# Pool mixer of a hybrid encoder layer: its weights folded into the input projection on the chip, the running means stored directly

## The chip, the cores and the metric

The kernel runs on one core of one Trainium2 chip, in one launch. The metric is device time in microseconds (us), as the median of several runs; the profile shows one more execution, with its own time. A core has five engines that the text names: TensorE (PE, with its weight loads PEld), VectorE (DVE), ScalarE (ACT), GpSimd (POOL) and SyncE (SP), which only issues transfers here. They run side by side and wait for each other through semaphores.

## What is computed

One layer on 16 + 1024 tokens of width 1024. A normalised input goes through one input projection, whose columns feed three mixers: a pool mixer (256 columns, four groups of 64, windows 2, 4, 8 and 16), forgetting attention (six heads) and stick-breaking attention (six heads). Their outputs are joined, pass an output projection, and a SwiGLU block follows. The pool mixer, which the change is about, is this:

```python
def multiscale_pool_mixer(u, pool_w, pool_scale):
    ...
    window_sum = cs - cs0[:, lo, jnp.arange(N_POOL_GROUPS)[None, :]]
    mean = window_sum / (t1 - lo).astype(jnp.float32)[None, :, :, None]
    d = (mean - ug).astype(u.dtype)
    mixed = jnp.einsum('blgc,gcd->blgd', d, pool_w)
    return mixed.reshape(b, l, POOL_WIDTH) * pool_scale
```

Here u is the projection's first 256 columns, u = a @ w_in[:, :256], and the running mean and the difference act along the tokens, each column for itself. So mixing the columns with pool_w, a 64 x 64 matrix per group, can be done after the running mean or before it.

## The kernel before

All large products run in a split form: each operand is kept as a high part (rounded to the matmul's input type, float32r) and a low part (the rest), and three matmuls (high x high, high x low, low x high) stand for one. A weight block of 128 output columns comes in four parts of 128 x 2 x 128: `wpart` (L158) loads one from DRAM over SP's queue (tile wr), POOL writes the high part (wh, through `hi_pool`, L76) and, for this part of the kernel, POOL also subtracts to get the low part (wl, L164). The tags wh and wl have five buffers each (WB = 5). `proj_piece` (L283) projects up to 512 tokens with 24 matmuls into PSUM (tag mm, two buffers), eight steps of the contraction times three.

Two streams are interleaved by hand. `attention` goes through six pairs of heads (the first stick-breaking, then three forgetting, then two stick-breaking), and `filler` gives TensorE work beside it: for each next pair the projections of its keys, queries and values (`project`, L365). In front of the projections for pairs 2 and 4 (POOLS, L847) it runs `pool_pieces` (L597) for one half of the pool mixer, two groups of 64 columns. Every step of a stream yields a planned cost, and `interleave` (L788) brings the filler to a goal (a sum of such costs) by the end of each pair. Both streams only write a program order; the planner of the tile framework then fixes each engine's order by that priority and by when, in its own time model, operands and buffers come free. The attention has its priority raised by 300 instructions (BOOST, L846).

One half of the pool mixer goes like this. The four weight parts are loaded; pw, a 128 x 128 tile of tag e, is cleared (L601), gets two 64 x 64 blocks of pool_w by transfer (L603), and is split into pwh (ACT, L605) and pwl (VectorE, L607). Then for four pieces of 248 to 264 tokens: projection into PSUM; u = projection times the row factor rbc (VectorE, L627), with 16 tokens of overlap carried along by POOL (L626, L630); the window sums by repeated doubling (VectorE, L639), each level in a new buffer of tag e; mean minus u, one instruction for each group of 64 partitions (VectorE, L647), into tag r; its high part on POOL and its low part on VectorE (L652). One piece later `mix` follows: three matmuls with pwh, pwl (L612 to L614), a copy on ACT that applies the pool scale (L616), and the store of the result to DRAM from ACT's queue (L617). Tags e and r have three buffers each; the stick-breaking attention (`sb_scores`, L442) uses the same two tags for every piece of its scores.

Of the kernel before, what the change touches and what calls it, by code (L numbers as in the profile page):

```python
# [8 lines left out]
F32 = mybir.dt.float32  # L9
# [7 lines left out]
KD = 8  # L17
NM = 16
# [12 lines left out]
def hymba_trunk(  # L31
# [5 lines left out]
    w_fl: bass.AP,  # L37
    fbias: bass.AP,
    pool_w: bass.AP,
    pool_scale: bass.AP,  # L40
# [77 lines left out]
    psc = cst.tile([128, 2], F32, name="psc")  # L118
    nc.scalar.dma_start(psc, pool_scale)
    fb = cst.tile([6, 1], F32, name="fb")  # L120
    nc.scalar.dma_start(fb, fbias)
# [35 lines left out]

    def wpart(c, hf):  # L158
        raw = T(r1, [128, 2, 128], F32, "wr", 4)
        nc.sync.dma_start(raw, w_in[c, :, 2 * hf:2 * hf + 2, :])  # L160
        wh = T(r1, [128, 2, 128], F32R, "wh", WB)
        hi_pool(wh, raw)
        wl = T(r1, [128, 2, 128], F32R, "wl", WB)
        WPE[0].tensor_tensor(wl, raw, wh, ALU.subtract)  # L164
        return wh, wl
# [6 lines left out]
    def wload(c):  # L172
        return wflat([wpart(c, hf) for hf in range(4)])
# [422 lines left out]

    def pool_pieces(ci):  # L597

        w = wload(ci)
        pw = T(ap_, [128, 512], F32, "e", 3)[:, :128]  # L600
# [5 lines left out]
        pwl = T(ap_, [128, 128], F32R, "pwl")  # L606
        V.tensor_tensor(pwl, pw, pwh, ALU.subtract)  # L607
        late = []

        def mix(s0, n, dh, dl):  # L610
            p = mm("mm", [128, 512], MMB)
            PE.matmul(p[:, :n], pwh, dh[:, :n], start=True, stop=False)  # L612
            PE.matmul(p[:, :n], pwh, dl[:, :n], start=False, stop=False)
            PE.matmul(p[:, :n], pwl, dh[:, :n], start=False, stop=True)  # L614
            yo = T(ap_, [128, 512], F32, "e", 3)
            S.activation(yo[:, :n], p[:, :n], AF.Copy, scale=psc[:, ci:ci + 1])  # L616
            nc.scalar.dma_start(ysd[ci][:, s0:s0 + n], yo[:, :n])  # L617

        last = T(ap_, [128, NM], F32, "last")
        for t0, m in ((0, 264), (248, 280), (512, 272), (768, 272)):  # L620
# [4 lines left out]
            if t0:  # L625
                G.tensor_copy(u[:, :NM], last)  # L626
            V.tensor_tensor(u[:, c0:m], o[0][:, :m - c0], rbc[:, t0 + c0:t0 + m], ALU.mult)  # L627
            if t0 + m < L:
                last = T(ap_, [128, NM], F32, "last")
                G.tensor_copy(last, u[:, m - NM:m])  # L630

            lv = []
            cur = u
            for lev in range(4 if ci else 2):
                sft = 1 << lev
                st = 2 * sft - 1
                nx = T(ap_, [128, 512], F32, "e", 3)
                lo = 64 if lev == (3 if ci else 1) else 0
                V.tensor_tensor(nx[lo:128, st:m], cur[lo:128, st:m], cur[lo:128, st - sft:m - sft], ALU.add)  # L639
                cur = nx  # L640
                lv.append(nx)
            n = m - NM
            dd = T(ap_, [128, 512], F32, "r", 3)
            for g in range(2):
                win = 2 << (2 * ci + g)
                r = slice(64 * g, 64 * g + 64)
                V.scalar_tensor_tensor(dd[r, :n], lv[-2 + g][r, NM:m], 1.0 / win, u[r, NM:m],  # L647
                                       ALU.mult, ALU.subtract)
            dh = T(ap_, [128, 512], F32R, "r", 3)
            hi_pool(dh[:, :n], dd[:, :n])  # L650
            dl = T(ap_, [128, 512], F32R, "r", 3)
            V.tensor_tensor(dl[:, :n], dd[:, :n], dh[:, :n], ALU.subtract)  # L652
            while late:
                mix(*late.pop())
            late.append((t0, n, dh, dl))
            yield 0.5
        while late:
            mix(*late.pop())
        yield 0.5

# [519 lines left out]
```

## Time and profile before

| | |
|---|---|
| median of 3 runs | 1284.89 us (1284.74 to 1286.3) |
| profiled execution | 1286.02 us, of which the span of the trace is 1284.2 us |
| busy time in the span | PE 1215.3 us, PEld 1023.5, DVE 947.2, ACT 630.5, POOL 480.2 |
| granted TensorE clock, mean | 0.982 of full speed |
| transfers | 147.13 MB, on average 115 GB/s |

All rows come from the one profiled execution. Times in its rows count from the start of the span. A matmul's busy time overlaps the next one's, so the distance from one start to the next is its price where they follow closely. The granted clock is TensorE's: 1 is 2.4 GHz, and its lower level is half of that, 1.2 GHz; a stretch's number is the mean over it.

### The profile page before, as it was taken

How to read it: one execution, taken by the hardware profiler on the slowest of the kernel's cores; microseconds unless marked ns; L12 is line 12 of the kernel's file. 1: busy time of each engine (PE TensorE's matmuls, PEld its weight loads, DVE VectorE, ACT ScalarE, POOL GpSimd, SP SyncE). 2: the span in 40 equal slices, each digit the busy share in tenths (PEclk: the TensorE clock that was granted, in tenths of full speed). 3: DMA queues.
4: the chain of work that ended last, by engine and by line, in shares of the span. 5: the costliest groups of instructions: out<-in, count | busy, mean ns of one | idle time of the engine just before them, and what ended most of it. 6: DMA issues, size and time to landing. Idle time of an engine off the chain costs nothing.

```text
span 1284.2 us, 18471 instructions
## 1 busy us (share of the span) xinstructions
PE 1215.3 (95%) x6310; PEld 1023.5 (80%) x6310; DVE 947.2 (74%) x1713; ACT 630.5 (49%) x1318; POOL 480.2 (37%) x534
## 2 busy tenths in 40 slices
PE   7699899999898989999898999999999999999997
PEld 5587778888788878778687888888888888788885
DVE  8667886868977779997777676666767656876557
ACT  6456754645448677767743333332223334444443
POOL 6459046362363764550105453443544410000001
PEclk9999899999899989999999999999999999999999
DMA  5100011010100161201505554445544439565653
GB/s 180 40 17 27 13 47 34 26 42 18 50 29 30 38 213 67 74 25 50 197 25 180 171 167 151 138 136 181 189 164 160 136 131 344 172 212 199 197 173 139
DMA packets 73146, 147.13 MB, mean 115 GB/s; under 512 B 9052, under 2 KB 21340, under 8 KB 73052
## 3 DMA queue, kind: packets, MB, share of 16 engines
q1 hardware_dynamic: 69728, 142.01, 33.3%
q10 hardware_dynamic: 3324, 3.95, 0.9%
q8 instruction: 50, 0.82, 0.3%
q14 instruction: 44, 0.36, 0.1%
HBM read 103.98 MB, written 41.94 MB: 114 GB/s over the span
## 4 chain that ended last, share of the span: by engine, by line
PE 66%; DVE 11%; issue 4%; ACT 4%; DMA 2%; POOL 1%; SPq 0%; DVEq 0%; POOLq 0%; ACTq 0%
PE s L890 21%; PE mm L289 10%; PE mm L890 8%; PE s L1075 7%; PE mm L701 4%; PE o L511 4%; PE mm L1075 3%; PE o L1075 3%; PE s L531 3%; DVE r L470 3%; PE s L429 1%; PE s L431 1%; DVE x L703 1%; DVE P L472 1%; DMA raw<-in_w_down 1%
## 5 line engine op out<-in xcount | busy, mean ns | idle before, releaser
L890 PE MATMUL s<-t,wh 128*128 128x512 f32 x544 | 170.4, 392 | 3.5 <-ACT wh L876 3.5
L890 PEld LDWEIGHTS s<-t,wh 128*128 128x128 f32 x544 | 102.7, 189 | 25.7 <-ACT wh L876 4.2
L890 PE MATMUL s<-s,wh 128*128 128x512 f32 x384 | 118.5, 390 | 0.0
L876 ACT CAST wh<-ss 128x512 fp32r<-128x512 f32 x80 | 49.5, 621 | 133.6 <-PE s L890 93.0
L890 PE MATMUL s<-t,wl 128*128 128x512 f32 x272 | 106.3, 391 | 0.0
L289 PE MATMUL mm<-x,wh 128*128 128x512 f32 (+1 forms) x320 | 100.1, 387 | 1.1 <-DVE pt L354 1.1
L538 ACT CAST ph<-s 128x512 fp32r<-128x512 f32 (+2 forms) x168 | 70.7, 434 | 60.0 <-PE s L531 23.9
L890 PE MATMUL mm<-t,wh 128*128 128x512 f32 x320 | 98.5, 389 | 0.0
L1063 ACT CAST wh<-sg 128x512 fp32r<-128x512 f32 x74 | 46.0, 623 | 104.6 <-PE s L1075 46.1
L876 ACT CAST wh<-raw 128x512 fp32r<-128x512 f32 x68 | 41.7, 621 | 111.2 <-PE s L890 72.4
L539 DVE TENSOR_TENSOR pl<-s,ph 128x512 fp32r<-128x512 f32 (+2 forms) x168 | 81.1, 492 | 19.9 <-ACT ph L538 17.5
L1064 DVE TENSOR_TENSOR wl<-sg,wh 128x512 fp32r<-128x512 f32 x74 | 51.0, 690 | 56.9 <-ACT wh L1063 56.6
L511 PE MATMUL o<-pl,v 128*128 128x256 f32 (+1 forms) x288 | 85.8, 314 | 0.7 <-DVE pl L521 0.6
L511 PE MATMUL o<-ph,v 128*128 128x256 f32 (+1 forms) x288 | 80.2, 292 | 3.8 <-ACT ph L520 2.4
L890 PEld LDWEIGHTS s<-s,wh 128*128 128x128 f32 x384 | 71.9, 188 | 14.9
L984 DVE TENSOR_TENSOR cg<-s,tmp 128x512 f32<-128x512 f32 x60 | 41.2, 687 | 56.9 <-PE s L890 56.9
L1114 POOL TENSOR_TENSOR r<-r,mhalf 128x1 f32<-128x1 f32 x8 | 4.4, 547 | 209.0 <-DVE r L1113 207.4
L289 PE MATMUL mm<-xa,wh 128*128 128x264 f32 (+3 forms) x248 | 78.5, 320 | 1.2 <-ACT rbc L239 0.7
L289 PE MATMUL mm<-xa,wl 128*128 128x264 f32 (+3 forms) x248 | 76.5, 313 | 1.2 <-POOL wl L164 1.2
L289 PE MATMUL mm<-xb,wh 128*128 128x264 f32 (+3 forms) x248 | 77.0, 313 | 0.0
L531 PE MATMUL s<-ident,P 128*128 128x128 f32 x432 | 68.8, 278 | 6.3 <-DVE pl L521 3.6
L878 DVE TENSOR_TENSOR wl<-ss,wh 128x512 fp32r<-128x512 f32 x80 | 68.7, 862 | 8.2 <-ACT wh L876 6.8
(287 smaller groups left out, 3636.6 us busy)
## 6 DMA issues: line engine op xcount, KB each, us to landing
sg<-lsd SPq DMA_DIRECT2D x70, 256.0 KB, 3.2
raw<-in_w_gate SPq DMA_DIRECT2D x22, 512.0 KB, 5.4
raw<-in_w_up SPq DMA_DIRECT2D x22, 512.0 KB, 3.9
wr<-in_w_in SPq DMA_DIRECT2D x80, 128.0 KB, 2.2
raw<-in_w_down SPq DMA_DIRECT2D x20, 512.0 KB, 3.6
lsd<-cg SPq DMA_DIRECT2D x40, 256.0 KB, 3.2
raw<-rsd SPq DMA_DIRECT2D x40, 256.0 KB, 3.4
raw<-in_w_down SPq DMA_DIRECT2D x34, 256.0 KB, 3.1
```

The source lines that it names most:

```text
L289: PE.matmul(p[:, :n], w[k][ww], xx(k, t0, n), start=i == 0, stop=i == 23)
L511: PE.matmul(po[:, c:256], pr.v[h][:, kb, :], x, start=first and ix == 0, stop=(kb == nkb - 1 and ix == 1), skip_group_check=True)
L531: PE.transpose(tp[:, gi, ii, :], ptiles[ii][:, kc], ident)
L538: S.copy(ph[:, a:b], tpf[:, a:b])
L539: V.tensor_tensor(pl[:, a:b], tpf[:, a:b], ph[:, a:b], ALU.subtract)
L701: PE.matmul(p, y_[:, ts_], w_[:, ds], start=i == 0, stop=i == 3 * len(ws) - 1)
L876: S.copy(wh, a)
L878: V.tensor_tensor(wl, a, wh, ALU.subtract)
L890: PE.matmul(p, ws[ww][:, k, :], xs_[xx][:, k, :], start=first and i == 0, stop=i == 11, skip_group_check=True)
L1063: S.copy(wh, a)
L1064: V.tensor_tensor(wl, a, wh, ALU.subtract)
L1075: PE.matmul(p, x[xx][:, 128 * b:128 * b + 128], y[yy], start=first and i == 0, stop=last and i == 2, skip_group_check=True)
```

## The change

The pool weights are multiplied into the projection's weights on the chip, once per half, before anything is projected. For that the host lays the first 256 columns of w_in down a second time, turned (w_pt: the 128 columns of a half on the partitions). `pool_weights` loads the four turned parts with `wpart`, splits them as before, and multiplies each 128 x 128 block with the split block-diagonal pw: 24 matmuls of 128 columns. ACT and VectorE split the products from PSUM into the wh and wl parts that `proj_piece` takes. The pieces then project straight to the mixed columns. The pool scale is applied in the first step on u. The last doubling, which only the upper 64 partitions need, is done in place, read and written backwards. One instruction with a per-partition reciprocal width (invw, four small fills at the start) gives mean minus u for all 128 partitions, and its result, in tag r, is stored from ACT's queue one piece later. The mixing matmuls, the split of their input (POOL and VectorE) and ACT's copies go.

```diff
+    invw = cst.tile([128, 2], F32, name="invw")
+    for ci in range(2):
+        for g in range(2):
+            V.memset(invw[64 * g:64 * g + 64, ci:ci + 1], 1.0 / (2 << (2 * ci + g)))
...
-    def wpart(c, hf):
+    def wpart(c, hf, src=None):
         raw = T(r1, [128, 2, 128], F32, "wr", 4)
-        nc.sync.dma_start(raw, w_in[c, :, 2 * hf:2 * hf + 2, :])
+        nc.sync.dma_start(raw, (w_in if src is None else src)[c, :, 2 * hf:2 * hf + 2, :])
...
-    def pool_pieces(ci):
-
-        w = wload(ci)
+    def pool_weights(ci):
+
         pw = T(ap_, [128, 512], F32, "e", 3)[:, :128]
         V.memset(pw, 0.0)
         for g in range(2):
...
         V.tensor_tensor(pwl, pw, pwh, ALU.subtract)
+        parts = []
+        for q in range(2):
+            turned = [wpart(ci, 2 * q + i, w_pt) for i in range(2)]
+            p = mm("mm", [128, 512], MMB)
+            for i in range(2):
+                th, tl = turned[i]
+                for k in range(2):
+                    for x, (tt, pp) in enumerate(((th, pwh), (th, pwl), (tl, pwh))):
+                        PE.matmul(p[:, 256 * i + 128 * k:256 * i + 128 * k + 128], tt[:, k, :], pp,
+                                  start=x == 0, stop=x == 2, skip_group_check=True)
+            for i in range(2):
+                pv = p[:, 256 * i:256 * i + 256].rearrange("p (a b) -> p a b", a=2)
+                wh = T(r1, [128, 2, 128], F32R, "wh", WB)
+                S.copy(wh, pv)
+                wl = T(r1, [128, 2, 128], F32R, "wl", WB)
+                V.tensor_tensor(wl, pv, wh, ALU.subtract)
+                parts.append((wh, wl))
+            yield 0.8
+        pr_w[ci] = wflat(parts)
+
+    pr_w = {}
+
+    def pool_pieces(ci):
+
+
+        yield from pool_weights(ci)
+        w = pr_w[ci]
         late = []
-
-        def mix(s0, n, dh, dl):
-            p = mm("mm", [128, 512], MMB)
-            PE.matmul(p[:, :n], pwh, dh[:, :n], start=True, stop=False)
-            PE.matmul(p[:, :n], pwh, dl[:, :n], start=False, stop=False)
-            PE.matmul(p[:, :n], pwl, dh[:, :n], start=False, stop=True)
-            yo = T(ap_, [128, 512], F32, "e", 3)
-            S.activation(yo[:, :n], p[:, :n], AF.Copy, scale=psc[:, ci:ci + 1])
-            nc.scalar.dma_start(ysd[ci][:, s0:s0 + n], yo[:, :n])
...
-            V.tensor_tensor(u[:, c0:m], o[0][:, :m - c0], rbc[:, t0 + c0:t0 + m], ALU.mult)
+            V.scalar_tensor_tensor(u[:, c0:m], o[0][:, :m - c0], psc[:, ci:ci + 1], rbc[:, t0 + c0:t0 + m],
+                                   ALU.mult, ALU.mult)
...
-                nx = T(ap_, [128, 512], F32, "e", 3)
-                lo = 64 if lev == (3 if ci else 1) else 0
-                V.tensor_tensor(nx[lo:128, st:m], cur[lo:128, st:m], cur[lo:128, st - sft:m - sft], ALU.add)
-                cur = nx
-                lv.append(nx)
+                if lev < (3 if ci else 1):
+                    nx = T(ap_, [128, 512], F32, "e", 3)
+                    V.tensor_tensor(nx[:, st:m], cur[:, st:m], cur[:, st - sft:m - sft], ALU.add)
+                    cur = nx
+                else:
+                    r = slice(64, 128)
+                    V.tensor_tensor(cur[r, st:m][:, ::-1], cur[r, st:m][:, ::-1],
+                                    cur[r, st - sft:m - sft][:, ::-1], ALU.add)
             n = m - NM
-            dd = T(ap_, [128, 512], F32, "r", 3)
-            for g in range(2):
-                win = 2 << (2 * ci + g)
-                r = slice(64 * g, 64 * g + 64)
-                V.scalar_tensor_tensor(dd[r, :n], lv[-2 + g][r, NM:m], 1.0 / win, u[r, NM:m],
-                                       ALU.mult, ALU.subtract)
-            dh = T(ap_, [128, 512], F32R, "r", 3)
-            hi_pool(dh[:, :n], dd[:, :n])
-            dl = T(ap_, [128, 512], F32R, "r", 3)
-            V.tensor_tensor(dl[:, :n], dd[:, :n], dh[:, :n], ALU.subtract)
+            yo = T(ap_, [128, 512], F32, "r", 3)
+            V.scalar_tensor_tensor(yo[:, :n], cur[:, NM:m], invw[:, ci:ci + 1], u[:, NM:m], ALU.mult, ALU.subtract)
             while late:
-                mix(*late.pop())
-            late.append((t0, n, dh, dl))
+                nc.scalar.dma_start(*late.pop())
+            late.append((ysd[ci][:, t0:t0 + n], yo[:, :n]))
             yield 0.5
-        while late:
-            mix(*late.pop())
-        yield 0.5
+        nc.scalar.dma_start(*late.pop())
+        yield 0.1
...
+        ("w_pt", wmain[:, :256].reshape(KD, 128, 2, 128).transpose(2, 3, 0, 1)),
```

## Rows read from the trace of the kernel before

**Rows 1.** The page: busy time by engine, and the chain's shares.

```profile
PE 1215.3 (95%) x6310; PEld 1023.5 (80%) x6310; DVE 947.2 (74%) x1713; ACT 630.5 (49%) x1318; POOL 480.2 (37%) x534
...
PE 66%; DVE 11%; issue 4%; ACT 4%; DMA 2%; POOL 1%; SPq 0%; DVEq 0%; POOLq 0%; ACTq 0%
```

**Rows 2.** Stretches: length, busy us (instructions) of each engine, granted clock, DMA share, GB/s.

```profile
134.00:160.00 26.00, 22.88 (x162) 21.55 (x162) 22.73 (x48) 18.66 (x47) 3.18 (x8) 0.90 0.02 7
290.00:312.00 22.00, 22.00 (x165) 20.50 (x165) 17.88 (x62) 13.15 (x37) 5.99 (x11) 1.00 0.08 25
312.00:338.00 26.00, 19.76 (x143) 17.42 (x143) 24.55 (x68) 13.16 (x30) 11.94 (x21) 0.99 0.09 31
338.00:345.00 7.00, 6.70 (x30) 5.89 (x30) 6.31 (x17) 1.99 (x5) 0.40 (x1) 0.56 0.17 57
...
160.00:200.00 40.00, 36.73 (x239) 31.96 (x238) 33.39 (x99) 21.66 (x54) 21.64 (x37) 0.96 0.16 51
```

**Rows 3.** TensorE in order of time: start, length, line, idle before, what ended it.

```profile
156.19 0.39 PE L612 MATMUL mm<-r,pwh 128*128 128x264 f32 x1 [0.98 <-POOL r L77]
...
337.82 0.90 PE L531 MATMUL s<-ident,P 128*128 128x128 f32 x3 [3.61 <-DVE pl L521]
...
341.12 0.41 PE L511 MATMUL o<-pl,v 128*128 128x256 f32 x1
341.34 0.41 PE L511 MATMUL o<-ph,v 128*128 128x256 f32 x1
```

**Rows 4.** VectorE lines: times in ns (min/median/max), or us and mean ns.

```profile
L647 DVE SCALAR_TENSOR_TENSOR r<-e,pt x16: 399/422/848, 146.7 to 343.8; 64x256 f32<-64x256 f32 x8, 64x248 f32<-64x248 f32 x4, 64x264 f32<-64x264 f32 x4
...
L652 DVE TENSOR_TENSOR r<-r,r x8: 410/416/887, 150.2 to 346.1; 128x256 fp32r<-128x256 f32 x4, 128x248 fp32r<-128x248 f32 x2, 128x264 fp32r<-128x264 f32 x2
...
L348 DVE TENSOR_TENSOR v<-mm,v 128x256 fp32r<-128x256 f32 x6 | 2.5, 416 | 0.0
```

**Rows 5.** TensorE in order of time: matmuls of 256 and 128 columns, transposes.

```profile
317.39 0.28 PE L511 MATMUL o<-pl,v 128*128 128x256 f32 x1
317.51 0.22 PE L511 MATMUL o<-ph,v 128*128 128x128 f32 x1
317.57 0.28 PE L511 MATMUL o<-pl,v 128*128 128x128 f32 x1
...
332.36 0.27 PE L517 MATMUL s<-ident,P 128*128 128x128 f32 x1
...
332.47 0.93 PE L531 MATMUL s<-ident,P 128*128 128x128 f32 x7
```

**Rows 6.** Half 0: clearing pw, its low part, last weight part, first projection.

```profile
L601 DVE MEMSET e<- x2: 165/165/165, 137.7 to 181.8; 128x128 f32 x2
...
141.72 0.28 DVE L607 TENSOR_TENSOR pwl<-e,pwh 128x128 fp32r<-128x128 f32 x1
...
127.59 0.73 POOL L164 TENSOR_TENSOR wl<-wr,wh 128x256 fp32r<-128x256 f32 x1
...
133.89 0.53 PE L289 MATMUL mm<-xa,wh 128*128 128x264 f32 x1
```

**Rows 7.** Half 1: the last weight part and the first projection matmul.

```profile
302.96 0.74 POOL L164 TENSOR_TENSOR wl<-wr,wh 128x256 fp32r<-128x256 f32 x1
...
305.45 0.37 PE L289 MATMUL mm<-xa,wh 128*128 128x264 f32 x1
```

**Rows 8.** A VectorE addition beside a POOL subtraction, and the next addition.

```profile
333.36 0.86 POOL L164 TENSOR_TENSOR wl<-wr,wh 128x256 fp32r<-128x256 f32 x1
...
333.55 0.96 DVE L639 TENSOR_TENSOR e<-e 128x265 f32<-128x265 f32 x1
...
334.61 0.43 DVE L639 TENSOR_TENSOR e<-e 64x257 f32<-64x257 f32 x1
```

**Rows 9.** VectorE scans: forwards (L278) and backwards (L470), us and mean ns.

```profile
L470 DVE TENSOR_TENSOR_SCAN r<-e,r 128x456 f32<-128x456 f32 x7 | 9.2, 1317 | 1.3 <-ACT e L467 1.3
...
L278 DVE TENSOR_TENSOR_SCAN cb<-P 6x1040 f32<-6x1040 f32 x1 | 2.8, 2842 | 0.6 <-POOL P L277 0.6
```

More of the change, by code (lines that the diff above doesn't have):

```diff
@@ L38, in hymba_trunk @@
     fbias: bass.AP,
+    w_pt: bass.AP,
     pool_w: bass.AP,
@@ L630, in pool_pieces @@
                 G.tensor_copy(last, u[:, m - NM:m])
-            lv = []
             cur = u
```

## The prediction

> **What bounds the kernel now.** I read the page first: TensorE is busy for 95% of the span and holds 66% of the chain that ended last, VectorE 11% [rows 1]. An average like that says "TensorE-bound", but the change touches only the two halves of the pool mixer (c = 0 and c = 1), so the second view is the table by stretches around them [rows 2]. Half 0 has its first projection matmul at 133.9 us, half 1 at 305.5 us [rows 6, 7]. Just ahead of half 1, from 290 to 312 us, TensorE is busy for 22.00 of 22.00 us. Then, in the 26 us in which half 1 is processed (312 to 338), it turns round: VectorE is busy for 24.55 us and TensorE for 19.76, and the 7 us after it run at a granted clock of 0.56 [rows 2]. Half 0 (134 to 160) looks alike: VectorE 22.73 of 26, TensorE 22.88, part of it at the lower clock (mean 0.90). So each half has a stretch of its own in which VectorE sets the pace, and both lie between stretches where TensorE does. Third, the order of time on TensorE shows what the reader should see there: at 337.82 it had stood idle for 3.61 us, waiting for a VectorE subtraction of the attention (L521) that stood in VectorE's queue behind the pool's instructions, and at 156.19 for 0.98 us in front of the mixing matmul L612, waiting for POOL's split of the mixer's input [rows 3].
>
> **Part 1: what leaves VectorE and POOL.** In each half there are four pieces of some 256 columns. Per piece, two 64-partition instructions on L647 become one on 128 partitions, and the subtraction on L652 goes; POOL's split goes as well. The medians are 0.42 us for either [rows 4], and a 128-partition form costs by its columns, so a piece saves 0.42 + 0.42 = 0.84 us of VectorE and a half 3.4. Inside 312 to 338 lie six of half 1's eight L647 and two of its four L652: 3 x 0.42 + 2 x 0.42 = 2.1 us saved where VectorE is full, and I count them all. Inside 134 to 160 lie four L647 and two L652 of half 0: 2 x 0.42 + 2 x 0.42 = 1.7 us, and the wait of 0.98 us at 156.19 loses its cause (no mixing matmul stands in TensorE's queue any more, and no POOL step ahead of it); I count half of it, since the attention matmul behind it would have waited for VectorE anyway: 2.2 us together. What is late next is, in both places, the attention's own chain through VectorE.
>
> The first step on each piece becomes a scalar_tensor_tensor with the pool scale in it; the same columns, taken at no cost. The last doubling becomes an in-place addition read and written backwards. No addition of that form is in the trace; the nearest rows are the scans, 2842 ns for 1040 columns forwards (2.73 ns each) and 1317 ns for 456 backwards (2.89 ns each) [rows 9]. A backward step is at worst some 6% dearer there, so I take it at nothing; the bound is eight additions of 0.43 us, 0.2 us, and a gain is excluded because the columns stay the same.
>
> **Part 2: what is added.** Per half, 24 matmuls of 128 columns make the product, four ACT copies and four VectorE subtractions split it; 12 mixing matmuls of some 256 columns and four ACT copies leave. The loads are as many and as large as before, only from the turned weights, and POOL splits them as before. Price of a 128-column matmul: at full clock one follows another after 0.06 us (317.51 to 317.57), one of 256 columns takes 0.12 (317.39 to 317.51), while a run of seven transposes, each with its own weight load, takes 0.93 us, of which a single one's own length is 0.27: (0.93 - 0.27) / 6 = 0.11 each [rows 5]. The new ones each load their weights too, so I take 0.11: 24 x 0.11 = 2.6 us against 12 x 0.12 = 1.4 us, net +1.2 us; the ends are 24 x 0.06 - 1.4 = 0 and, if the mixing matmuls had been hidden anyway, +2.6. For half 1 the product falls into the stretch where TensorE has no idle time [rows 2]: +1.2 us on the path. For half 0, TensorE is idle for 3.1 us of 134 to 160: nothing, and 1.2 if that cover is gone.
>
> The Trainium skill, "TensorE: Matmul & The Clock Gate", section "Back-to-back issue gap", speaks against cutting a product into 128-column matmuls: a stream with a weight load each is said to settle at about 81 ns for 128 columns, well above what the columns alone ask for. The trace agrees in direction (0.11 in the run of transposes, 0.06 for a single pair [rows 5]). An estimate from the page's figure, 24 x 0.081 - 1.4, would put +0.5 us where the sum has +1.2.
>
> The new subtractions read PSUM, as L348 does, which takes 416 ns at this size [rows 4]: 4 x 0.42 = 1.7 us per half. For half 1 they come before the first projection, where VectorE has 22 - 17.88 = 4.1 us of idle time [rows 2]: nothing, at most 1.7. For half 0 it depends on the next term. The four small fills of the new reciprocal widths are bounded by four of the 0.17 us fill on L601 [rows 6], 0 to 0.7 us at the start; taken at nothing, as no load and no other step stands between them and their use, over 100 us later.
>
> **Part 3: the new chain.** This is the term I am least sure of. The block-diagonal pool weights (pw) were needed only by the mixing matmul; now nothing of a half can start without them. They live in a buffer of tag e, of which there are three, and the stick-breaking attention, which has the higher priority, asks for the same ones. In half 0 pw was cleared only at 137.7, loaded, copied, and its low part was there at 141.72 + 0.28 = 142.0 us, while the projection's weights were ready at 127.59 + 0.73 = 128.3 and the projection ran from 133.89 [rows 6]. If pw comes no earlier, the first product ends at 142.0 + 12 x 0.11 = 143.3, and with a copy and a subtraction (0.4 each) the first projection starts at about 144.1, 10 us later. Two pieces (48 matmuls x 0.12 = 5.9 us of TensorE) then move behind 144. The idle time of TensorE in 134 to 160 and 160 to 200 is 3.1 + 3.3 = 6.4 us [rows 2], so it could take them in, and VectorE's pool work moves out of its full stretch in exchange. Bounds: 0 and +5.9. I take +1.5, nearer to 0 because of this idle time. In half 1 pw is there long before (the second fill on L601 is at 181.8 [rows 6]); its chain runs from the weights (302.96 + 0.74 [rows 7]) through matmul, copy and subtraction, some 2 to 4 us, during which the attention has work for TensorE: 0.
>
> **What moves between queues.** The eight stores stay on ACT's queue and still go out one piece late; they now wait for a VectorE result that is a piece old, not for ACT's own copy, so the attention's exponentials behind them are not held up: nothing. Only the last store of a half follows its instruction at once, and can hold ACT for about one VectorE step, 0.4 us; also off the path. On SP, the load of pw now comes before the loads of the turned weights in the program; while it waits for the clearing of pw, loads behind it wait too, but they are of no use before pw is there, so this lies inside the bound of part 3. The planner's account of the filler grows by 1.6 - 0.4 = 1.2 units per half against fixed goals, so the boundaries of the attention's pairs meet the filler 1.2 and later 2.4 units further back. That is work moved by as much, not added: nothing, with an end of 1.2 either way that the bounds of parts 2 and 3 already span.
>
> **Part 4: the clock.** After the idle 3.61 us TensorE ran at 0.56 from 338 to 345; the 256-column matmuls stand 0.22 us apart there (341.12 to 341.34) against 0.12 [rows 3, 5], so 7.0 x (1 - 0.56) = 3.1 us were lost. If part 1 takes 2.1 us off that idle time, 1.5 remain; whether the clock still falls the trace doesn't tell, so between 0 and 3.1 I take half, -1.6.
>
> **The sum.** Half 1: -2.1 - 1.6 + 1.2 = -2.5. Half 0: -2.2 + 1.5 = -0.7. Together -3.2 us. The profiled execution took 1286.02 us (span 1284.2), so 1282.8; it lies 1.1 us above the median of the runs shown (1284.89), which gives 1281.7 on the scale of the medians. A difference under 0.2% (2.6 us) can't be told from none for this kernel, so this is a small gain just outside. The forecast's own range: -7.4 (all of the clock, product and chain at their lower ends) to -2.6, so 1277.5 to 1282.3.
>
> **The rivals.** First, the gain is eaten: the clock falls all the same and the late pw costs 3 us instead of 1.5: -2.1 + 1.2 - 2.2 + 3 = -0.1, so 1284.8. For it: the clock also fell in half 0's stretches, where the single waits are shorter than 3.61 us [rows 2, 3]. Against it: it needs two terms to go badly.
>
> Second, slower: pw is late in half 0 and TensorE has nothing to put in its place. Then the 5.9 us lie in later stretches that are full, VectorE's saving of 2.2 falls where TensorE sets the pace and is worth nothing, and the four subtractions (1.7) come when VectorE is full: half 0 costs up to 5.9 + 1.7 = 7.6, with half 1 at -2.5 that is +5.1, so up to 1290; it decides for "slower" once two thirds of the 7.6 show, about 1288. For it: pw's row at 137.7 and the two pieces that stood ahead of it. Against it: the idle 6.4 us.
>
> Third, the gain is larger. Next to POOL's instructions VectorE's get longer: an addition on L639 took 0.96 us beside POOL's subtraction at 333.36 [rows 8], where some 0.43 is usual for its columns. Eight splits on POOL leave, of 0.40 us each, so at most 3.2 us more come back: 1278.5. The Trainium skill, "SBUF — State Buffer", section "SBUF: two separate sides", says that VectorE with two SBUF inputs and GpSimd take a shared port pair as a whole and in turn, and the trace agrees with that at 333.55. Against the rival: POOL's other splits, the 0.8 us ones that stand in that row, stay.
>
> **Chances and range.** Forecast 0.35, third rival 0.07, first rival 0.30, slower 0.28. So faster 0.42, same 0.30, slower 0.28. The range takes in the larger gain and the slower case: 1277 to 1290.
>
> **What would show it.** Right: the 16 instructions on L647 become 8 and the 8 on L652 become 8 on PSUM ahead of the pieces, no 3.6 us idle stretch at half 1's end, a clock near 1 after it. Part 3 is wrong if half 0's first projection starts before about 138 us, and the slower rival is right if it starts after 143 and TensorE's idle time from 112 to 200 grows by over 4 us. The forecast falls if the clock still drops after half 1, or if the stretch from 290 to 345 gets no shorter.

## The result, and the profile after

The changed kernel takes 1292.6 us (median of 4 runs, 1290.4 to 1293.49) against 1285.34 us of the kernel before on the same chip (1284.74 to 1286.3): a ratio of 1.0049, interval 1.0037 to 1.0061. It is slower by 0.5%, outside the predicted range (1277 to 1290). Its profiled execution took 1293.49 us, with a span of 1291.7 us. Differences in us below are (ratio - 1) x 1285.3, so that runs beside different repetitions of the kernel before can be compared; the change as a whole is +6.3 us (4.8 to 7.8; the two medians alone differ by 7.3).

From here on a row's line number is that of its own kernel: what was L890 in the kernel before is L906 after, L289 is L295, L601 is L606. First the page of after, to be held against [rows 1]: busy time by engine, the chain's shares, and two groups of the feed-forward block's products.

```profile
PE 1229.0 (95%) x6334; PEld 1028.0 (80%) x6334; DVE 944.7 (73%) x1709; ACT 628.5 (49%) x1318; POOL 474.4 (37%) x526
...
PE 75%; DVE 14%; ACT 4%; issue 2%; POOL 2%; DMA 2%; SPq 0%; DVEq 0%; POOLq 0%; ACTq 0%
...
L906 PE MATMUL s<-t,wh 128*128 128x512 f32 x544 | 174.1, 398 | 3.4 <-ACT wh L892 3.4
...
L906 PE MATMUL s<-s,wh 128*128 128x512 f32 x384 | 118.8, 391 | 0.8 <-DVE cg L1000 0.8
```

VectorE and GpSimd have 2.5 and 5.8 us less to do (the prediction's terms add up to 3.4 and 3.2), but TensorE is busy for 13.7 us more with only 24 matmuls more. The second view is the same stretches as in [rows 2] (length, busy us of PE, PEld, DVE, ACT and POOL, granted clock, DMA share, GB/s), of after:

```profile
134.00:160.00 26.00, 21.45 (x126) 19.45 (x127) 18.75 (x39) 17.36 (x44) 4.57 (x8) 0.74 0.04 13
160.00:200.00 40.00, 40.00 (x284) 36.80 (x283) 34.39 (x98) 20.66 (x52) 23.68 (x39) 1.00 0.18 58
290.00:312.00 22.00, 21.18 (x150) 19.01 (x148) 18.08 (x65) 14.29 (x43) 2.59 (x5) 1.00 0.02 7
312.00:338.00 26.00, 24.92 (x192) 22.84 (x191) 25.35 (x78) 15.91 (x38) 8.32 (x16) 1.00 0.09 31
338.00:345.00 7.00, 7.00 (x62) 6.94 (x62) 5.88 (x20) 2.88 (x8) 4.04 (x9) 1.00 0.30 97
```

Half 1 went the way I forecast, and further: TensorE is busy for 24.92 of the 26 us (19.76 before), the 7 us behind them run at a clock of 1.00 (0.56 before), and no idle time of 3.6 us is left. Half 0 went the other way: 134 to 160 lost TensorE time and clock (0.74, before 0.90). But neither is where the microseconds went. That shows in a third view, the first and last start of the feed-forward products (min/median/max ns of one, then first and last start in us), first of before, then of after:

```profile
L890 PE MATMUL s<-t,wh x544: 388/389/632, 653.0 to 1052.7; 128*128 128x512 f32 x182
L890 PE MATMUL s<-s,wh x384: 387/389/482, 623.4 to 1063.3; 128*128 128x512 f32 x192
```

```profile
L906 PE MATMUL s<-t,wh x544: 388/396/628, 650.8 to 1060.3; 128*128 128x512 f32 x182
L906 PE MATMUL s<-s,wh x384: 389/389/501, 621.2 to 1071.1; 128*128 128x512 f32 x192
```

The first of these products starts 2.2 us earlier than before (621.2 against 623.4), so up to there the change has won 2.2 us. The last one starts 7.8 us later (1071.1 against 1063.3). Ten microseconds go in a block in which the change touches no line. And only one of the two groups got longer: 389 to 396 ns where the moving operand is a tile of tag t, 389 in both where it has tag s. In order of time the step from one matmul to the next shows it best; of before, then of after, at about the same time:

```profile
821.23 0.39 PE L890 MATMUL s<-s,wl 128*128 128x512 f32 x1
821.46 0.39 PE L890 MATMUL s<-t,wh 128*128 128x512 f32 x1
821.69 0.39 PE L890 MATMUL s<-t,wl 128*128 128x512 f32 x1
821.91 0.62 PE L890 MATMUL s<-t,wh 128*128 128x512 f32 x2
822.37 0.39 PE L890 MATMUL s<-t,wl 128*128 128x512 f32 x1
```

```profile
823.27 0.39 PE L906 MATMUL s<-s,wl 128*128 128x512 f32 x1
823.49 0.62 PE L906 MATMUL s<-s,wh 128*128 128x512 f32 x2
823.95 0.39 PE L906 MATMUL s<-s,wl 128*128 128x512 f32 x1
824.17 0.40 PE L906 MATMUL s<-t,wh 128*128 128x512 f32 x1
824.41 0.40 PE L906 MATMUL s<-t,wl 128*128 128x512 f32 x1
824.64 0.63 PE L906 MATMUL s<-t,wh 128*128 128x512 f32 x2
825.11 0.40 PE L906 MATMUL s<-t,wl 128*128 128x512 f32 x1
```

Before, four matmuls on t take from 821.46 to 822.37, 228 ns each by these rounded starts (227 as the median over all); after, four on s take from 823.27 to 824.17 (225 each), and four on t from 824.17 to 825.11 (235). There are 544 + 272 + 320 + 160 = 1296 matmuls with t as their moving operand. Over all of their records, pauses left out, the mean step is 226.7 ns before and 233.5 after: 1296 x 6.8 ns = 8.8 us. (The expectations below go by 226 and 234 ns, and by 8 ns for the difference.)

What can the change have to do with it? It adds one tile, invw, of 128 partitions and 8 bytes each, among the constants. A tile takes 32 bytes of a partition there, and everything that is placed after it on that side of SBUF moves up by 32 bytes: the weights (wh, wl) of the feed-forward products and tag s, but not tag t, which is placed from the other side. My theory from here on: the tile's place, not its work, costs the 8 to 10 us, and the rest of the change is worth about -2. The rival: the pool mixer's new form itself delays what follows (the slower rival of the prediction).

### The profile page after: what moved, and what is told of

Same layout as the page of the kernel before. It is cut to its first block, busy times and chain, and to the rows that moved or that the text cites. A ratio compares the mean times of both kernels' runs of the same rounds, so it can differ in the third digit from the quotient of the medians.

```text
span 1291.7 us, 18497 instructions
## 1 busy us (share of the span) xinstructions
PE 1229.0 (95%) x6334; PEld 1028.0 (80%) x6334; DVE 944.7 (73%) x1709; ACT 628.5 (49%) x1318; POOL 474.4 (37%) x526
## 4 chain that ended last, share of the span: by engine, by line
PE 75%; DVE 14%; ACT 4%; issue 2%; POOL 2%; DMA 2%; SPq 0%; DVEq 0%; POOLq 0%; ACTq 0%
PE s L906 24%; PE mm L295 12%; PE s L1091 9%; PE mm L906 8%; PE o L517 4%; PE mm L717 4%; DVE r L476 4%; PE mm L1091 3%; PE o L1091 3%; PE s L537 3%; DVE P L478 1%; PE s L435 1%; PE s L437 1%; DVE x L719 1%; ACT e L467 1%
## 5 line engine op out<-in xcount | busy, mean ns | idle before, releaser
L906 PE MATMUL s<-t,wh 128*128 128x512 f32 x544 | 174.1, 398 | 3.4 <-ACT wh L892 3.4
L906 PEld LDWEIGHTS s<-t,wh 128*128 128x128 f32 x544 | 102.5, 189 | 29.3 <-ACT wh L892 4.1
L906 PE MATMUL s<-s,wh 128*128 128x512 f32 x384 | 118.8, 391 | 0.8 <-DVE cg L1000 0.8
L906 PE MATMUL s<-t,wl 128*128 128x512 f32 x272 | 108.2, 398 | 0.0
L295 PE MATMUL mm<-x,wh 128*128 128x512 f32 (+1 forms) x320 | 99.8, 385 | 2.2 <-DVE pt L360 2.2
L906 PE MATMUL mm<-t,wh 128*128 128x512 f32 x320 | 100.6, 396 | 0.0
L906 PEld LDWEIGHTS s<-s,wh 128*128 128x128 f32 x384 | 71.9, 188 | 16.3 <-DVE cg L1000 1.2
L295 PE MATMUL mm<-xa,wh 128*128 128x264 f32 (+3 forms) x248 | 78.0, 319 | 0.7 <-ACT rbc L245 0.7
L295 PE MATMUL mm<-xa,wl 128*128 128x264 f32 (+3 forms) x248 | 76.7, 316 | 1.2 <-POOL wl L170 1.2
L295 PE MATMUL mm<-xb,wh 128*128 128x264 f32 (+3 forms) x248 | 76.1, 311 | 0.0
L1091 PE MATMUL s<-wl,wh 128*128 128x512 f32 x192 | 74.7, 389 | 0.0
```

What stands on the lines that cost most here:

```text
L295: PE.matmul(p[:, :n], w[k][ww], xx(k, t0, n), start=i == 0, stop=i == 23)
L906: PE.matmul(p, ws[ww][:, k, :], xs_[xx][:, k, :], start=first and i == 0, stop=i == 11, skip_group_check=True)
L1091: PE.matmul(p, x[xx][:, 128 * b:128 * b + 128], y[yy], start=first and i == 0, stop=last and i == 2, skip_group_check=True)
```

## Experiments: the tile

### e1_before_left32

The kernel before, with nothing but a tile of 32 bytes where invw would be, and one fill of it. The rest of its instructions and their order on each engine are those of the kernel before.

```diff
+    gap = cst.tile([128, 8], F32, name="gap")
+    V.memset(gap, 0.0)
```

> The kernel before, unchanged but for one unused 32-byte tile among the constants where the change puts invw (cleared once); every tile allocated after it on that side of SBUF moves up by 32 bytes, the tiles on the other side (among them tag t of the FFN's first products) stay. Theory A (addresses): the 1296 matmuls that read a moving operand of tag t beside weights of tag wh or wl follow each other after 234 ns in place of 226, 8 ns each, so about +10 us, near 1295. Theory B (the pool mixer's new chain, or its work, costs the 7 us): no change, 1285.

Measured: 1294.05 us, ratio 1.0073 (1.0055 to 1.0091), +9.4 us. The groups of its products from 690 to 1060 us, by form (busy us, mean ns; before has 389 for both):

```profile
L892 PE MATMUL s<-t,wh 128*128 128x512 f32 x464 | 147.4, 396 | 0.0
...
L892 PE MATMUL s<-s,wh 128*128 128x512 f32 x304 | 93.7, 389 | 0.0
```

An unused tile costs at least as much as the whole change did, in the same group of matmuls.

### e2_after_no_shift

The changed kernel with invw in two spare columns of the tile of the pool scale, which takes 32 bytes either way; so nothing moves.

```diff
-    psc = cst.tile([128, 2], F32, name="psc")
-    nc.scalar.dma_start(psc, pool_scale)
+    psc = cst.tile([128, 4], F32, name="psc")
+    nc.scalar.dma_start(psc[:, 0:2], pool_scale)
...
-    invw = cst.tile([128, 2], F32, name="invw")
+    invw = psc[:, 2:4]
```

> The changed kernel whole, with invw in the unused 24 bytes behind the pool scale, so that no tile of the kernel before moves. Theory A: the 8 ns go, and what is left is the attention part's gain of some 2.8 us that the two traces show at the end of the attention: about 1282. Theory B: still 1292.

Measured: 1285.14 us (12 runs), ratio 0.9996 (0.9982 to 1.0009), -0.5 us, and the group on t is back at 389 ns:

```profile
L906 PE MATMUL s<-t,wh 128*128 128x512 f32 x461 | 143.6, 389 | 0.0
```

From both sides, then: the place of the tile costs 6.8 us in the changed kernel (6.3 + 0.5) and 9.4 in the kernel before, and the pool mixer's new form by itself makes no difference that can be measured.

### Place or distance: e4, e5, e6, e7, e10

What about the place does it? e4 leaves the constants as they were and puts the 32 bytes between the pool of the feed-forward weights and the pool with tag s.

```diff
     wp = ctx.enter_context(pool("wp"))
+    gp = ctx.enter_context(pool("gp"))
+    gap = T(gp, [128, 8], F32, "gap")
+    V.memset(gap, 0.0)
     e1 = ctx.enter_context(pool("e1"))
```

> The kernel before with an unused 32-byte tile between the pool of the split weights (tags wh, wl) and the pool of tag s, the moving operands on the weights' side: the weights and tag t stay where they were, tag s moves by 32 bytes. If the price comes from the distance between the weights' and the moving operand's addresses, the matmuls with a moving operand of tag s (576) go to 234 ns and those with tag t stay at 226: +4.6 us, near 1290. If tag t itself, or its side, is what is slow, nothing changes: 1285.

Measured: 1290.33 us, 1.004 (1.0025 to 1.0055), +5.1 us, and the slow group has changed sides:

```profile
L893 PE MATMUL s<-t,wh 128*128 128x512 f32 x464 | 144.7, 390 | 0.0
L893 PE MATMUL s<-s,wh 128*128 128x512 f32 x304 | 95.5, 395 | 0.0
```

Now tag s has moved against the weights, and t has not. So it is the distance between the moving operand and the weights' pool that counts, and 384 + 192 = 576 matmuls on s pay: their mean step is 233.4 ns, before 226.9, which makes 3.8 us. It isn't the place of one operand alone, either: by the build, s starts at 69888 bytes in e1 and in e4 and is slow only in e4, and t at 147424 in the kernel before and in e1 and is slow only in e1.

e5 moves both sides by 32 bytes, e6 the one side by 128, e7 one side by 32 and the other by 96, and e10 the one side by 256. All are the kernel before with an unused tile (e5 and e7 with two). e5:

```diff
+    rg = ctx.enter_context(pool("rg", side="right"))
+    gap2 = rg.tile([128, 8], F32, name="gap2")
+    V.memset(gap2, 0.0)
...
+    gap = cst.tile([128, 8], F32, name="gap")
+    V.memset(gap, 0.0)
```

> The kernel before with 32 unused bytes on both sides, so that weights, tag s and tag t all move by 32 bytes and keep their distances modulo 64. If the distance counts: 1285, all products at 226 ns. If the absolute address of the weights or of the left side counts: slow as with the left side alone, near 1295.

e6 is e1 with another size, and e7 is e5 with a larger gap2:

```diff
+    gap = cst.tile([128, 32], F32, name="gap")
```

> The kernel before with 128 unused bytes among the constants: weights and tag s move by 128 bytes, tag t stays. Runs so far: distance between the moving operand and the weights a multiple of 128 bytes, 226 ns; 32, 64 or 96 bytes off, 234 ns. If the rule repeats every 128 bytes: 226 ns for all products and 1285. If it repeats every 256 bytes or more: 234 ns for tag t and near 1295.

```diff
+    gap2 = rg.tile([128, 24], F32, name="gap2")
```

> The kernel before with 32 unused bytes on the weights' side and 96 on the other (which is filled downwards): weights, tag s and tag t all start at a multiple of 128 bytes, where all stood 96 bytes behind one before. Distances stay multiples of 128. If the distance counts, and not where each operand stands: 226 ns for all products, 1285. If the place itself counts: 234 ns somewhere, 1290 to 1295.

```diff
+    gap = cst.tile([128, 64], F32, name="gap")
```

> The kernel before with 256 unused bytes among the constants: weights and tag s move by 256 bytes, tag t stays, so the distance of tag t to the weights changes by 256. If the price is free of cost at every multiple of 256 bytes: 226 ns for all products and 1285. If only the old distance is: 228 to 237 ns for tag t and near 1294.

e5 was a miss: I had wanted to keep the distance, but the other side is filled downwards, so the two shifts add up (-32 - 32) instead of cancelling. It is useful all the same, as another distance. The distances follow from where the build puts the tiles (weights at 37088 bytes, s at 69856, t at 147424 in the kernel before); the step is the median from one start to the next:

| kernel | distance of t, modulo 256 | step on t, ns | distance of s, modulo 256 | step on s, ns | ratio to before | us |
|---|---|---|---|---|---|---|
| before | 0 | 227 | 0 | 227 | 1 | |
| after | 224 | 234 | 0 | 227 | 1.0049 | +6.3 |
| e1 | 224 | 234 | 0 | 227 | 1.0073 | +9.4 |
| e4 | 0 | 227 | 32 | 234 | 1.004 | +5.1 |
| e5 | 192 | 233 | 0 | 227 | 1.0071 | +9.1 |
| e6 | 128 | 229 and 238 in turn, mean 233 | 0 | 227 | 1.0055 | +7.1 |
| e7 | 128 | 229 and 238 in turn, mean 233 | 0 | 227 | 1.0054 | +6.9 |
| e10 | 0 | 227 | 0 | 227 | 1.0003 | +0.4 |

The group on t in e6, to be held against the 389 ns of the kernel before:

```profile
L892 PE MATMUL s<-t,wh 128*128 128x512 f32 x464 | 147.2, 395 | 0.0
```

e7 has all these tiles at multiples of 128 bytes and is as slow as e6, so it isn't the alignment of one tile by itself; e10 moves the weights by 256 bytes and is as fast as the kernel before (0.9993 to 1.0012). Its groups:

```profile
L892 PE MATMUL s<-t,wh 128*128 128x512 f32 x464 | 144.3, 389 | 0.0
L892 PE MATMUL s<-s,wh 128*128 128x512 f32 x312 | 96.1, 389 | 0.0
```

Among the feed-forward products of these kernels, the 512-column matmul is free of the loss only where the moving operand and the weights lie a multiple of 256 bytes apart in the partition. The partner could be TensorE's weight load or another access to that pool (its raw tiles); the runs don't tell these apart.

## Experiments: the pool mixer without the shift

e2 has the tile out of the way and is worth nothing, though half 1 got better. So where does its gain go? From here on every kernel with the new form has e2's place of invw.

### e8_half0_only and e9_half1_only

The new form in one half; the other half keeps the old pool_pieces (as pool_before, the code of the kernel before).

```diff
-                    yield from pool_pieces(ci)
+                    yield from (pool_pieces if ci == 0 else pool_before)(ci)
```

(e9: ci == 1.)

> The changed kernel without the 32-byte shift, and with the new form for half 0 alone; half 1 goes as in the kernel before. Theory of the prediction: half 0 gains little or loses, because its product waits for pw: between -0.7 and +5 us at the end of the attention. Rival: the late projections of half 0 cost nothing, since TensorE has idle time up to 200 us: within 1 us of the kernel before there.

> The changed kernel without the 32-byte shift, and with the new form for half 1 alone; half 0 goes as in the kernel before. The prediction gave half 1 -2.5 us; the trace of the changed kernel is 8 us ahead of the kernel before by 350 us. If half 1 alone makes that: 5 to 8 us ahead at 350 us here too, and some 2.5 to 4 of it left at the end of the attention, near 1282. If half 0's shorter work makes it: nothing here.

Measured: half 0 alone 1289.08 us (10 runs), 1.0019 (1.001 to 1.0029), +2.4 us; half 1 alone 1268.86 us, 0.986 (0.9845 to 0.9875), -18.0 us. The halves together give -0.5, not -15.6. So half 0 loses, half 1 wins seven times what I forecast, and the two together lose about 15 us that neither loses alone.

### e12_both_early_pw

Why half 0 loses, in rows of the changed kernel: VectorE, POOL and TensorE in order of time.

```profile
136.86 0.17 DVE L606 MEMSET e<- 128x128 f32 x1
141.91 0.28 DVE L612 TENSOR_TENSOR pwl<-e,pwh 128x128 fp32r<-128x128 f32 x1
```

```profile
145.70 0.41 POOL L78 TENSOR_SCALAR wh<-wr 128x256 fp32r<-128x256 f32 x1 [11.17 <-PE mm L621]
146.08 2.09 POOL L170 TENSOR_TENSOR wl<-wr,wh 128x256 fp32r<-128x256 f32 x2
```

```profile
147.78 0.28 PE L621 MATMUL mm<-pwh,wl 128*128 128x128 f32 x1
...
151.39 0.30 PE L621 MATMUL mm<-pwh,wh 128*128 128x128 f32 x1
...
155.25 0.41 PE L621 MATMUL mm<-pwl,wh 128*128 128x128 f32 x1
155.46 0.47 PE L295 MATMUL mm<-xa,wh 128*128 128x264 f32 x1
```

pw is cleared at 136.86, its low part comes at 141.91, as in [rows 6]. From there to the end of the product 13 us pass, where I had counted 2.1 (12 matmuls, a copy and a subtraction). The part I had not seen is the second row: POOL, which splits the turned weights, stands for 11.17 us until the product's first matmuls free a buffer, since the product's operands and its results come from the same five buffers of tags wh and wl. Most of that wait is the late pw once more: it began at 134.5, and pw's low part was there only at 142.2. The first projection starts at 155.46, not 144.1.

e12 takes pw out of tag e, into the weights' own tag wr:

```diff
-        pw = T(ap_, [128, 512], F32, "e", 3)[:, :128]
+        pw = T(r1, [128, 2, 128], F32, "wr", 4)[:, 0, :]
```

> Both halves in the new form, no shift, with pw in a buffer of tag wr, which only the filler uses, in place of tag e. If the wait for a buffer of tag e is what makes half 0 late: pw is cleared some 10 us earlier, half 0's first projection runs before 145 us in place of 155, and TensorE is idle less between 112 and 160 us; by the prediction's step that is worth up to 5.9 us. If lateness costs nothing: same time at the end of the attention as both halves without it, 1285.

Measured: 1277.72 us, 0.9935 (0.992 to 0.9951), -8.4 us, that is 7.9 better than e2. pw is cleared 46 us earlier, POOL's wait of 11.17 us is gone although the buffers are the same five, and the first projection starts at 139.03. (The move also leaves tag e to the attention; e12 does not tell that apart from the earlier clearing.)

```profile
91.16 0.17 DVE L606 MEMSET wr<- 128x128 f32 x1
```

```profile
133.27 0.28 PE L621 MATMUL mm<-pwh,wh 128*128 128x128 f32 x1
133.38 0.28 PE L621 MATMUL mm<-pwl,wh 128*128 128x128 f32 x1
133.49 0.27 PE L621 MATMUL mm<-pwh,wl 128*128 128x128 f32 x1
133.60 0.27 PE L621 MATMUL mm<-pwh,wh 128*128 128x128 f32 x1
...
139.03 0.29 PE L295 MATMUL mm<-xa,wh 128*128 128x264 f32 x1
```

The stretch from 112 to 160 us, of e2 and then of e12, shows the price: TensorE's busy time 40.18 against 42.02, and its clock, as a mean between its two levels, 0.82 against 0.96. The idle time differs by 1.8 us only; 0.14 of the clock over 48 us is an estimated 6.7 us at full speed, so most of the price is the clock.

```profile
112.00:160.00 48.00, 40.18 (x229) 33.81 (x228) 37.84 (x80) 32.64 (x85) 16.57 (x20) 0.82 0.06 19
```

```profile
112.00:160.00 48.00, 42.02 (x287) 36.76 (x287) 41.46 (x88) 33.99 (x92) 16.56 (x21) 0.96 0.07 23
```

### e11_both_goals, e13_before_goals, e14_both_early_pw_goals

The planned costs of the pool mixer's filler grew by 1.2 units per half, and the goals by which attention and filler are matched stayed. Added up from the code, the goal of the fourth pair is 166.4 units, and the last turn of the values' projection in front of it (project 4) ended at 164.56 in the kernel before. With one half in the new form it ends at 165.76, still under the goal. With both it would end at 166.96; the step before it ends at 166.46, past the goal, so the turn is left to the next pair. There it is still the first thing in the program order, but the first piece of the next projection, which in the kernel before stands ahead of that pair's first attention step, now stands behind it. The other pairs shift too: counted in steps of the code, e2's filler is 3, 1, 1, 3 and 2 steps behind that of the kernel before at the first attention step of pairs two to six (e8's 3, 1, 2, 1 and 1, e9's 0, 0, 0, 1 and 1). e11 raises the two goals by 1.2 each, and from the third pair on its filler stands where that of the kernel before does:

```diff
-    GOALS = (PC + 8, PC + 4, PC, PC + UC, PC - AHEAD + X4, X5)
+    GOALS = (PC + 8 + 1.2, PC + 4, PC, PC + UC + 1.2, PC - AHEAD + X4, X5)
```

> Both halves in the new form, no shift, and the goals of the hand-written interleaving raised by 1.2 for the first and the fourth pair, as much as the new halves add to the filler's account. If half 0 undoes half 1's gain because the filler falls 2.4 units behind the attention: like half 1 alone, 1268 to 1276. If it does so through its own late product and the planner's order after it: like both without this, 1285.

Measured: 1266.45 us, 0.9852 (0.9833 to 0.9872), -19.0 us, 18.5 better than e2. So what the two halves lost together comes back with the matching. But raised goals could be an improvement of their own, whatever the pool mixer does; e13 is the kernel before with the same goals.

> The kernel before with only the goals of the interleaving raised by 1.2 for the first and the fourth pair. If the 18 us that the raised goals gave with both halves in the new form come from the goals alone: near 1268 here. If they need the new form's shorter work: within 3 us of 1285.

Measured: 1281.69 us (10 runs), 0.9959 (0.9947 to 0.9971), -5.3 us. Of the 18.5 us, 5.3 were to be had before the change, and by subtraction about 13 belong to it. The 5.3 have a place: from 640 to 700 us, at the start of the feed-forward products, TensorE is busy for 56.46 of 60 us at a clock of 0.97 in the kernel before. The same stretch of e2, of e11 and of e13:

```profile
640.00:700.00 60.00, 56.05 (x243) 44.83 (x241) 44.44 (x43) 22.77 (x31) 14.92 (x10) 0.97 0.29 92
```

```profile
640.00:700.00 60.00, 60.00 (x266) 49.67 (x266) 44.93 (x46) 22.83 (x33) 22.98 (x15) 1.00 0.38 124
```

```profile
640.00:700.00 60.00, 60.00 (x270) 49.80 (x269) 46.62 (x46) 23.00 (x31) 16.64 (x11) 1.00 0.33 110
```

The idle time there goes in all kernels with raised goals, and in e9 too, whose goals are as before (60.00 of 60.00): what decides over it is open. Of the other 13 us some 9 lie in the attention: at its end, near 604 us, e11 is 13.1 us ahead of the kernel before by equal instructions (the start of the same matmul in both traces), e2 4.2. From 450 to 500 us, for one, TensorE is busy for 45.76 us in e2 and for 48.61 in e11. Where the last 4 lie, and which of the shifted steps makes the difference, was not followed further.

e14 has both edits, early pw and raised goals.

> Both halves in the new form, no shift, pw in a buffer of tag wr, and the raised goals. If the early pw (some 8 us) and the goals (some 18 us) act in separate places: near 1259. If they remove the same loss, or the planner's order undoes one: 1266 to 1278.

Measured: 1263.69 us (1261.56 to 1265.83), 0.982 (0.9793 to 0.9846), -23.1 us. That is the lowest time of these kernels, 1.8% below the kernel before and 2.3% below the change as made. With raised goals the early pw is worth 4.1 us (23.1 - 19.0), without them 7.9: the two seem to recover in part the same time. The intervals of e11 and e14 overlap, so the 4.1 rest on the traces as much: at the end of the attention e14 is 17.2 us ahead of the kernel before by equal instructions, e11 13.1.

## Why the prediction was wrong, and where it was right

**The step that failed** is the one on the four small fills of invw, "taken at nothing". As work they are nothing: four fills of 59 ns between 0.8 and 1.1 us. But the sum has no term for where the new tile lies. It moved the weights of the feed-forward products by 32 bytes against tag t, which costs 6.8 us by e2 against the change, 9.4 us by e1 and 8.8 us by the steps in the trace. Without it the change would have been at 1285.14 us, inside the range. I had gone through every engine, queue and buffer that the diff names; the cost was in a block that it doesn't name, and no row of the trace of before could show it, because there both distances were multiples of 256 bytes.

**Part 3, the late pw** had the right mechanism and the wrong size. I took +1.5 us, between 0 and 5.9, nearer to 0 "because of this idle time"; early pw gives back 7.9 us, or 4.1 with the goals raised. (Its upper end, 48 x 0.12, is 5.8 and not 5.9.) The idle time of 160 to 200 us did take projections in: TensorE is busy for 40.00 us there, before for 36.73. That of 134 to 160 did not (21.45, before 22.88): there the product waited for pw, and the splits for its second half stood behind it on POOL. The prediction's own test has two parts. The first, a first projection after 143, came out for the slower rival (155.46). The second did not: TensorE's idle time from 112 to 200 did not grow by 4 us, it went from 9.4 to 8.6. The stretch from 112 to 160, of before and then of after (160 to 200 stands in [rows 2] and in the second view of after):

```profile
112.00:160.00 48.00, 41.92 (x263) 36.90 (x264) 41.95 (x90) 33.84 (x88) 18.80 (x25) 0.89 0.07 24
```

```profile
112.00:160.00 48.00, 39.39 (x230) 33.55 (x231) 38.09 (x82) 33.31 (x86) 16.14 (x20) 0.86 0.06 18
```

What the late pw costs shows mostly in the granted clock instead (0.82 in e2, 0.96 in e12), and the sum has no clock term for half 0. Against the kernel before, half 0 as a whole costs 2.4 us (e8), not the 7.6 of that rival.

**The planner's account**, "work moved by as much, not added: nothing, with an end of 1.2 either way", is the second wrong step. Reading units of planned cost as microseconds that shift was wrong: 2.4 units left the filler one to three steps further back from the second pair on, and by subtraction some 13 us hung on that. Which of these steps it is, the runs don't show.

**Half 1** was right in kind: the idle 3.61 us of [rows 3] are gone and the clock behind is 1.00 (0.56 in [rows 2]). It was too small in size, at -2.5. Near 404 us, where both streams' matmuls show the same lead again, e9 is 5.6 us ahead of the kernel before by equal instructions, e8 1.5 behind and e2 4.7 ahead. So the new form is worth about 6 us in half 1's own stretch, and up to there the halves nearly add up. The other 12 us of e9's 18.0 come later, where the pool mixer has no work left, and so does what the two halves lose together. The forecast had no term for either.

And the reason was only half right. VectorE is as full as before in 312 to 338 (25.35 us, before 24.55). TensorE's own work also came later there: the product runs from 315.8 to 324.1, not in 290 to 312 where the sum had put it, and the first projection from 324.12, before from 305.45 [rows 7], so TensorE had projections to do while VectorE worked off the attention. e8 tells the two reasons apart, since its half 1 has the old form and is late too (first projection at 316.28). From 312 to 345 it keeps TensorE busy for 29.99 us at a clock of 0.95:

```profile
312.00:345.00 33.00, 29.99 (x225) 28.20 (x224) 30.94 (x91) 17.78 (x41) 9.77 (x20) 0.95 0.08 26
```

In the kernel before it is 26.5 us (19.76 + 6.70 [rows 2]), in after 31.9 at 1.00. So the later place alone fills more than half of the idle time, and the new form the rest and the clock.

**Durations** held. The product's matmuls stand 0.11 us apart (133.27 to 133.60 in e12), as taken from the transposes of [rows 5]. The Trainium skill, "TensorE: Matmul & The Clock Gate", section "Back-to-back issue gap", would have had 81 ns there; the trace has 110. The in-place doubling, backwards on 64 partitions, costs nothing extra, and the subtraction from PSUM is what L348 was [rows 4]. Two instructions are a little longer than those they replace: the first step with the scale in it (481 ns, 419 before) and the mean minus u on 128 partitions (477 against 422). In after, as times in ns (min/median/max):

```profile
L649 DVE SCALAR_TENSOR_TENSOR pt<-mm,psc,rbc x8: 458/481/493, 162.2 to 343.3; 128x264 f32<-128x264 f32 x4, 128x256 f32<-128x256 f32 x4
...
L665 DVE TENSOR_TENSOR e<-e x8: 417/434/472, 163.8 to 349.7; 64x269 f32<-64x269 f32 x2, 64x257 f32<-64x257 f32 x2, 64x261 f32<-64x261 f32 x1, 64x277 f32<-64x277 f32 x1
...
L669 DVE SCALAR_TENSOR_TENSOR r<-e,invw,pt x8: 367/477/656, 164.2 to 350.7; 128x256 f32<-128x256 f32 x4, 128x248 f32<-128x248 f32 x2, 128x264 f32<-128x264 f32 x2
...
L628 DVE TENSOR_TENSOR wl<-mm,wh x8: 409/421/425, 150.3 to 328.1; 128x256 fp32r<-128x256 f32 x8
```

**The rivals.** The time, 1292.6, is nearest to the slower rival's 1290, and half 0's projection is as late as that rival says. Yet it isn't the reason: with the late pw and without the shift (e2) the kernel is not slower. e2's 1285.14 is the first rival's 1284.8, but not by its terms either: half 1's gain was larger, half 0's loss was larger, and the matching took the rest, so that this time is met by luck. Nothing points to the third rival: VectorE's busy time fell by 2.5 us, not by more than the 3.4 of the terms.

## What to carry to other kernels

A new tile is an edit to the place of every tile behind it: put a small constant into spare bytes of one that is there, and when a change moves time in a block that it doesn't touch, compare the same group's mean duration in both traces first. An operand that becomes the head of a chain should not wait in a ring of buffers that another stream drains, and a chain whose inputs and outputs share one ring can wait for itself, as POOL did for 11.17 us when its head was late. Where an order is matched by planned costs, check the goals when a cost changes, by a run and not by the size of the change in microseconds.

## What the hardware showed

In this kernel's feed-forward block a 512-column matmul with a weight load each (float32r) follows the one before after 227 ns when its moving operand and the weights' tiles lie a multiple of 256 bytes apart in the partition (before, e10), and after 233 to 234 ns on average at distances of 32 (e4), 128 (e6, e7), 192 (e5) or 224 (e1, after) bytes modulo 256. The Trainium skill, "SBUF — State Buffer", section "Who interferes with whom", gives TensorE two independent read ports and says "PE and ACT never wait on anyone."; the measured steps of e1, e4 and e10 speak against this as a full account, and the measurement decides here. Outside that block the distance is not the whole account. The attention's 512-column projections (L289) stand 232 ns apart in the kernel before (median), nearly all with their moving operand 128 bytes off modulo 256; but the output projection's 512-column matmuls (L701) stand 231 ns apart there even where the distance is 0 (119 steps, at a granted clock of 1.00). What the 4 ns are there is open.
